# A hybrid decoder layer: two matmuls instead of three per weight tile in the mixer's projections by head, the halves copied by ScalarE and added by GpSimd

## The chip, the core and the metric

The kernel runs on one core of a Trainium2 chip. The metric is the device time of one execution in microseconds. Before the change it is 1942.86 us, the median of three runs (1942.37 to 1943.96).

## The reference

One layer with a sequence of T = 256 positions, model width D = 2048, heads of 128, eight attention heads ("fox") and eight recurrent heads ("gdn"):

```python
h = ada_in(x, norm_g[l, 0], sh1, sc1)                       # norm, scale and shift from c
x = x + 0.5 * gt1 * swiglu(h, gate_w[0], up_w[0], down_w[0])   # FFN 1
h = ada_in(x, norm_g[l, 1], sh2, sc2)
x = x + gt2 * hybrid_mixer(h, ...)                          # the mixer
h = ada_in(x, norm_g[l, 2], sh3, sc3)
x = x + 0.5 * gt3 * swiglu(h, gate_w[1], up_w[1], down_w[1])   # FFN 2
return rmsnorm(x, final_norm)

def hybrid_mixer(h, w_in, w_out, ...):
    q_f, k_f, v_f, f_f, qkv_g, a_g, b_g, z_g = split(h @ w_in)
    # fox: softmax(q k^T / sqrt(128) + decay(log_sigmoid(f_f))) @ v, then rmsnorm
    # gdn: qkv_g -> causal conv of width 4 -> silu -> q, k, v;
    #      q and k normed, gates from a_g and b_g,
    #      gated delta rule in chunks of 64 (a triangular solve per chunk), times silu(z)
    return concat(o_f, o_g) @ w_out
```

## The kernel before, in words

**Products.** The activations stand transposed, features on the partitions. Weights come from memory in blocks of eight tiles of 128x128 (one DMA of 512 KB, L121). Each number is split into a high and a low part: ScalarE (ACT) casts a block to `whi` (L123), VectorE (DVE) takes the rest, `wlo` (L135), each with four buffers. The activations are split likewise into halves HI and LO. A product is then high times high, plus high times low, plus low times high. In both FFNs and in the mixer's output projection most tiles are done by two matmuls: one of 512 columns, `whi` times both halves of the activations side by side (L481, L485), and one of 256, `wlo` times HI (L482, L486). In the mixer's projections by head, `project` (L760 to L773) does three matmuls of 256 columns per tile (L769, L770, L771) into the same 256 columns of a PSUM bank `pp`, and the sum of the three is there when the last has run. There are 41 such projections of 16 tiles, 656 tiles in all: gates, 8 keys, 16 queries and values of gdn, 16 queries and keys of fox. The projections Z and V run over rows instead (L782 to L784, three of 512 columns).

**Stages.** FFN 1 takes the span's first 738 us, the mixer runs to about 1235, FFN 2 to the end. The mixer starts with one `project` of four heads (64 tiles: gates and keys 0 to 2), and then follows a list written by hand, `ORDER`: K3 ... K7 Z0 V0 F0 G0 F1 G1 ... F7 (K keys, G the queries and values of a gdn head, F queries and keys of a fox head). Then comes the output projection (`po`, L485 and L486), and FFN 2.

**Small work.** Everything behind a projection is a generator: `gates`, `keys`, `decays`, `solve`, `gdn`, `fox`, `to_out`. Each stops at `yield n` and is taken up once the clock of `tick`, 0.35 us a tile, has moved on by n. So the places of its matmuls in PE's queue are fixed when the program is built, in tiles, and PE runs its queue in order: a small matmul whose input isn't ready holds all products behind it. A scheduler puts the instructions of each of the other engines in order, and these too run in that order.

**After a projection.** `conv_silu` (L915) copies `pp` into `cp` (ACT L918), scales it (ACT L919), adds three shifted taps (DVE L921) and applies silu (ACT L922). `gates` (L799) copies 24 rows (ACT L802); a matmul turns them (`pcol`, L811), DVE and ACT work on the result (L813 to L835), `prow` and `pcum` sum it (L844 to L853), ACT L855 copies the row sums, which go to memory (`rowd`) and come back spread over the partitions (`x<-rowd`, `rw<-rowd`). From these `decays` builds `Ln` (DVE L902, then eight exponentials on ACT, L905), which the last step of `keys` (DVE L947) multiplies. `keys` itself does transposes (`pk`, L934), products (`pkk`, L937), and then ACT L940 and L941, with PSUM tiles that the next head's `keys` uses again. `fox` gets its `qk` by two ACT copies (L1241).

Of the kernel before, what the change touches and what calls it, by code (L numbers as in the profile page):

```python
# [8 lines left out]
F32 = mybir.dt.float32  # L9
# [3 lines left out]
AF = mybir.ActivationFunctionType  # L13
ALU = mybir.AluOpType
PSUM = bass.MemoryType.PSUM

P = 128
D = 2048
T = 256
KD = D // P  # L20
# [5 lines left out]
NH = 8  # L26
HD = 128
# [3 lines left out]
GR = 24  # L31
# [44 lines left out]
def woven(ap):  # L76

    return ap.rearrange("p (a b) -> p b a", a=2)


def runs(ap):

    return ap.rearrange("p (a b) -> p a b", a=2)


def turns(ap):

    return ap.rearrange("p (b a) -> p a b", a=2)
# [61 lines left out]
def layer_kernel(ctx: ExitStack, tc: tile.TileContext, xrow, c, adaw, cols, cst, w, out, order, dbg=None):  # L150
    nc = tc.nc
    V, A, G, PE = nc.vector, nc.scalar, nc.gpsimd, nc.tensor
# [200 lines left out]
    LO, HI = 0, 1  # L353
# [312 lines left out]
    for kind, i in (("x", 0), ("x", 1), ("c", 0), ("c", 1), ("x", 2), ("x", 3), ("c", 2), ("c", 3)):  # L666
        with nullcontext() if hold is None else tc.issue_after(hold):
            if kind == "c":
                hold = cond(i)
            else:  # L670
                t, q = divmod(i, 2)
# [57 lines left out]
    def mixer():  # L729
# [30 lines left out]
        def project(items):  # L760

            pp = [psn(i, "pp") for i in range(len(items))]
            todo = [(i, k) for k in range(KD) for i in range(len(items))]
            for i, k in todo:
                m, n = items[i]
                h_need(k)
                wh, wl = W.next(m, k, n)
                hh, hl = woven(plain[:, k, HI]), woven(plain[:, k, LO])
                PE.matmul(pp[i][:, :T], wh, hh, start=(k == 0), stop=False)  # L769
                PE.matmul(pp[i][:, :T], wh, hl, start=False, stop=False)  # L770
                PE.matmul(pp[i][:, :T], wl, hh, start=False, stop=(k == KD - 1))  # L771
                tick(TILE_US)
            return [p_[:, :T] for p_ in pp]  # L773

        def project_rows(mat, grp):

# [22 lines left out]
        def gates(ps):  # L799

            yr = x[:, 8]
            A.copy(runs(yr[R]), turns(ps[R]))  # L802
            y, ny, e, em, t0, q = (x[:, j, : 2 * GR].rearrange("p (t r) -> p t r", t=2) for j in range(10, KD))
            coef = tiny.tile([P, GR + PAD["hid"]], F32, name="coef", bufs=1)[:, :GR]
            tc.keep_in_program_order(A.activation(coef, L("alog"), AF.Exp))
            V.tensor_scalar(coef, coef, -1.0, None, ALU.mult)
            yield 2.0
            pc = psf("pcol")
            pcv = pc[:, : 2 * GR].rearrange("p (t r) -> p t r", t=2)
            for t in range(2):  # L810
                PE.transpose(pcv[:, t], yr[R, t * P : (t + 1) * P], ident[R, :GR])  # L811
            both = lambda c_: c_.unsqueeze(1).to_broadcast([P, 2, GR])
            V.tensor_tensor(y, pcv, both(L("gbias")), ALU.add)  # L813
            V.tensor_tensor(y, y, both(C("sgn")), ALU.mult)
            V.scalar_tensor_tensor(ny, y, -1.0, y, ALU.mult, ALU.min)
            A.activation(e, ny, AF.Exp)
            V.tensor_scalar(em, y, 0.0, None, ALU.min)
            A.activation(em, em, AF.Exp)

            S = ny  # L820
            V.tensor_scalar(t0, e, 2.0, None, ALU.add)
            V.reciprocal(t0, t0)
            V.tensor_tensor(S, e, t0, ALU.mult)
            V.tensor_tensor(t0, S, S, ALU.mult)
            V.tensor_scalar(q, t0, 1.0 / 17.0, None, ALU.mult)
            for n in (15, 13, 11, 9, 7, 5, 3):
                V.scalar_tensor_tensor(q, q, 1.0 / n, t0, ALU.add, ALU.mult)
            V.scalar_tensor_tensor(q, q, 1.0, S, ALU.add, ALU.mult)
            V.tensor_scalar(y, y, 0.0, None, ALU.max)
            V.scalar_tensor_tensor(y, q, 2.0, y, ALU.mult, ALU.add)  # L830
            V.tensor_tensor(y, y, both(coef), ALU.mult)

            V.tensor_scalar(t0, e, 1.0, None, ALU.add)
            V.reciprocal(t0, t0)
            V.tensor_tensor(colS[:, :, 4], em[:, :, 16:24], t0[:, :, 16:24], ALU.mult)  # L835
            yield 8.0

            fox_, gdn_ = slice(0, NH), slice(NH, 2 * NH)
            pr = psf("prow")
            po = psf("pcum")  # L840
            pcs = po[:, : 6 * NH].rearrange("p (t q r) -> p t q r", t=2, q=3)
            for t in range(2):
                sl = slice(t * P, (t + 1) * P)
                PE.matmul(pr[:NH, T + t * P : T + (t + 1) * P], y[:, t, gdn_], C("tri64"), start=True, stop=True)  # L844
                PE.matmul(pr[:NH, sl], y[:, t, fox_], C("tri"), start=True, stop=(t == 0))
                if t:
                    PE.matmul(pr[:NH, sl], y[:, 0, fox_], L("ones"), start=False, stop=True)
            for t in range(2):
                PE.matmul(pcs[:, t, 1], C("tri64"), y[:, t, gdn_], start=True, stop=True)
                PE.matmul(pcs[:, t, 2], C("tru64"), y[:, t, gdn_], start=True, stop=True)  # L850
                PE.matmul(pcs[:, t, 0], C("tri"), y[:, t, fox_], start=True, stop=(t == 0))
                if t:
                    PE.matmul(pcs[:, t, 0], L("ones"), y[:, 0, fox_], start=False, stop=True)  # L853
            rt = x[:, 8:10].rearrange("p a t -> p (a t)")[:NH]
            A.copy(rt, pr[:NH])  # L855
            nc.sync.dma_start(rows, rt)
            V.tensor_copy(colS[:, :, 0:2], pcs[:, :, 0:2])
            A.activation(colS[:, :, 2:4], pcs[:, :, 1:3], AF.Exp)
            V.tensor_tensor(nbeg, colS[:, :, 4], colS[:, :, 2], ALU.mult)
            V.tensor_scalar(nbt, colS[:, :, 4], -1.0, None, ALU.mult)  # L860
            V.tensor_scalar(ng, colS[:, :, 1], -1.0, None, ALU.mult)
            yield 2.0
            fetch_rows(0)
            yield 1.0
# [50 lines left out]
        def conv_silu(ps, n, dst):  # L915
            cp, cv = pt("cp"), pt("cv")
            tap = lambda s: L("conv", 4 * n + s, 1)
            A.copy(runs(cp), turns(ps))  # L918
            A.activation(cv, cp, AF.Copy, scale=tap(3))  # L919
            for s in range(1, 4):  # L920
                V.scalar_tensor_tensor(cv[:, s:], cp[:, : T - s], tap(3 - s), cv[:, s:], ALU.mult, ALU.add)  # L921
            A.activation(dst, cv, AF.Silu)  # L922
# [3 lines left out]
        def keys(h):  # L926

            kT = kk[h].bitcast(F32)
            yield 3.0
            pk = pss("pk")  # L930
            pg = pss("pkk")
            for t in range(2):
                sl = slice(t * P, (t + 1) * P)
                PE.transpose(pk[:, sl], kT[:, 0, sl], ident)  # L934
            for t in range(2):
                sl = slice(t * P, (t + 1) * P)
                PE.matmul(pg[:, sl], kT[:, 0, sl], kT[:, 0, sl], start=True, stop=True)  # L937
            for t in range(2):
                j1 = tmp.tile([P, P], BF16, name="j1")
                A.activation(j1, pk[:, t * P : (t + 1) * P], AF.Square, accum_out=ssk[:, t, h : h + 1])  # L940
            A.copy(kT[:, 1], pk[:, :T])  # L941
            V.tensor_scalar(ssk[:, :, h], ssk[:, :, h], EPS, None, ALU.add)
            V.reciprocal(r2[:, :, h], ssk[:, :, h])
            nb2 = tiny.tile([P, 2], F32, name="nb2")
            V.tensor_tensor(nb2, nbt[:, :, h], r2[:, :, h], ALU.mult)
            for t in range(2):
                V.scalar_tensor_tensor(Ln[:, h, t], pg[:, t * P : (t + 1) * P], nb2[:, t : t + 1], Ln[:, h, t], ALU.mult, ALU.mult)  # L947
# [50 lines left out]
        def gdn(h):  # L998
# [1 line left out]
            kT, q_ = kk.pop(h).bitcast(F32), qv.pop(h).bitcast(F32)  # L1000
            dec, egb = ups.pop(h)
            L_, U = Ln[:, h], U0[:, h]
            yield 5.0 if h < NH - 2 else 3.0

            pv = pss("pvq")
            pg = pss("pkq")
# [136 lines left out]
        def fox(h, qk, vt):  # L1143
# [2 lines left out]
            for t, o, wd in ((0, 0, P), (1, P, T)):  # L1146
                A.activation(fm[:, o : o + wd], cb[:, :wd], AF.Identity, bias=colS[:, t, 0, h : h + 1], scale=-1.0)
            V.tensor_tensor(fm, fm, C("foxm"), ALU.add)
            yield 1.0
            pl = psf("plog")  # L1150
            for t, o, wd in ((0, 0, P), (1, P, T)):
                sl = slice(t * P, (t + 1) * P)
# [51 lines left out]
        def step(kind, h):  # L1204
# [25 lines left out]
            elif kind == "V":  # L1230
                finish("k", NH if h else 0)
                pv = project_rows("vf", h)
                vts[h] = [spare(4 * h), spare(4 * h + 2)]
                for t in range(2):
                    A.copy(vts[h][t], pv[t])
            else:
                pp = [project([(m, h)])[0] for m in ("qf", "kf")]
                finish("fox", h - 1)
                qk = spare(8 + 2 * (h % 2)).rearrange("p (a t) -> p a t", a=2)
                for i in range(2):  # L1240
                    A.activation(runs(qk[:, i]), turns(pp[i]), AF.Copy, scale=1.0 / math.sqrt(HD) if i == 0 else 1.0)  # L1241
                start("fox", h, fox(h, qk, vts[h // 4]))
                if h + 1 < NH:
                    rowf[h + 1] = row_of(h + 1, 0, "f")
# [200 lines left out]
```

## Time and profile before

| | us |
|---|---|
| median of three runs | 1942.86 (1942.37 to 1943.96) |
| the profiled execution | 1943.79 |
| its span | 1941.9, so 1.9 lie around the span |
| busy: PE, PE weight loads | 1903.0, 1777.2 |
| busy: DVE, ACT, GpSimd (POOL) | 1554.0, 1041.2, 56.8 |
| granted clock of TensorE | 0.992 |

The page gives busy time by engine, 40 slices of the span, the chain that ended last and the costliest groups of instructions. A group's line has the source line, the engine, the operation, output and inputs, the count, and then the busy time in us and the mean of one in ns; matmuls are pipelined, so the mean of one is longer than the distance from one start to the next. That distance is read from the timeline, whose first column is the start in us and whose second is the duration. A row of the waits names who waited, for whom, for how long in all, how often, and the longest.

### The profile page before, as it was taken

The numbers are of one execution on the slowest core, as the hardware profiler recorded it, in microseconds if no ns is written. First come the engines' busy times: TensorE is split into PE (matmuls) and PEld (weight loads), VectorE is DVE, ScalarE is ACT, GpSimd is POOL, SyncE is SP. The second block draws the span as 40 slices with busy tenths as digits, with TensorE's granted clock in tenths as the row PEclk, the third lists the DMA queues.
The fourth block names the chain that finished last, engine by engine and source line by source line (L and its number), as shares of the span: only waits on it lengthen the run. The fifth ranks groups of instructions, "written<-read, shape, count | busy, mean of one in ns | idle before, by whom it ended". The sixth has DMA issues, their size and how long they took to land. (4 is left out here: it accounts for less than half of the span.)

```text
span 1941.9 us, 33701 instructions
## 1 busy us (share of the span) xinstructions
PE 1903.0 (98%) x13087; PEld 1777.2 (92%) x13087; DVE 1554.0 (80%) x2415; ACT 1041.2 (54%) x1647; POOL 56.8 (3%) x55
## 2 busy tenths in 40 slices
PE   8999999999999999999999999999999999999998
PEld 6999999998999988889989998999999999999997
DVE  6999978989989997779987989976777665666654
ACT  6544555433455446858657655665554445555553
POOL 0000000000000030000000001100000000000011
PEclk8999999999999999999999999999999999999999
DMA  9989867999999975586667568667767665565663
GB/s 371 359 308 358 305 224 258 400 369 376 356 358 339 361 302 212 212 314 220 214 242 257 201 218 303 208 258 252 245 253 257 244 225 200 201 200 202 202 200 120
DMA packets 129490, 519.58 MB, mean 268 GB/s; under 512 B 18217, under 2 KB 21545, under 8 KB 111153
## 3 DMA queue, kind: packets, MB, share of 16 engines
q1 hardware_dynamic: 129330, 517.42, 72.9%
q8 instruction: 103, 1.69, 0.3%
q14 instruction: 57, 0.47, 0.1%
HBM read 512.89 MB, written 4.47 MB: 266 GB/s over the span
## 5 line engine op out<-in xcount | busy, mean ns | idle before, releaser
L135 DVE TENSOR_TENSOR wlo<-wraw,whi 128x1024 fp32r<-128x1024 f32 x674 | 822.3, 1226 | 268.3 <-ACT whi L123 267.3
L123 ACT CAST whi<-wraw 128x1024 fp32r<-128x1024 f32 x674 | 700.6, 1047 | 515.1 <-PE pd L485 166.5
L485 PE MATMUL pd<-hid,whi 128*128 128x512 f32 x1408 | 461.8, 382 | 0.0
L486 PE MATMUL pd<-hid,wlo 128*128 128x256 f32 x1408 | 384.6, 273 | 2.6 <-DVE wlo L135 2.6
L260 DVE CUSTOM_DVE_ANT_0 adat<-adat,cs,colt 128x2048 f32<-128x2048 f32 x140 | 329.2, 2351 | 6.5 <-DMA adat<-in_ada_dram 6.5
L481 PE MATMUL pg<-hs,whi 128*128 128x512 f32 x912 | 302.2, 382 | 0.5 <-DVE shc L432 0.5
L481 PE MATMUL pu<-hs,whi 128*128 128x512 f32 x912 | 302.2, 382 | 0.0
L485 PEld LDWEIGHTS pd<-hid,whi 128*128 128x128 f32 x1408 | 266.0, 189 | 36.9
L486 PEld LDWEIGHTS pd<-hid,wlo 128*128 128x128 f32 x1408 | 270.3, 192 | 5.4 <-DVE wlo L135 5.3
L567 PE MATMUL pgu<-hs,whi 128*128 128x256 f32 x896 | 245.8, 277 | 5.9 <-ACT hs L371 5.9
L482 PE MATMUL pu<-hs,wlo 128*128 128x256 f32 x912 | 249.2, 273 | 0.0
L482 PE MATMUL pg<-hs,wlo 128*128 128x256 f32 x912 | 248.9, 273 | 0.0
L569 PE MATMUL pgu<-hs,wlo 128*128 128x256 f32 x896 | 245.1, 278 | 2.4 <-DVE wlo L135 2.4
L568 PE MATMUL pgu<-hs,whi 128*128 128x256 f32 x896 | 246.5, 277 | 0.0
L481 PEld LDWEIGHTS pg<-hs,whi 128*128 128x128 f32 x912 | 172.4, 189 | 24.8 <-ACT shc L431 0.7
L481 PEld LDWEIGHTS pu<-hs,whi 128*128 128x128 f32 x912 | 172.4, 189 | 23.6
L769 PE MATMUL pp<-hs,whi 128*128 128x256 f32 x656 | 188.9, 289 | 1.6 <-ACT hs L375 1.6
L770 PE MATMUL pp<-hs,whi 128*128 128x256 f32 x656 | 182.9, 279 | 0.0
L771 PE MATMUL pp<-hs,wlo 128*128 128x256 f32 x656 | 182.7, 278 | 0.0
L567 PEld LDWEIGHTS pgu<-hs,whi 128*128 128x128 f32 x896 | 172.9, 194 | 6.7 <-ACT hs L371 6.3
L482 PEld LDWEIGHTS pu<-hs,wlo 128*128 128x128 f32 x912 | 175.0, 192 | 1.0 <-DVE wlo L135 0.9
L482 PEld LDWEIGHTS pg<-hs,wlo 128*128 128x128 f32 x912 | 175.1, 192 | 0.4
(337 smaller groups left out, 2593.8 us busy)
## 6 DMA issues: line engine op xcount, KB each, us to landing
wraw<-in_w_dram SPq DMA_DIRECT2D x674, 512.0 KB, 4.4
adat<-in_ada_dram SPq DMA_DIRECT2D x140, 1024.0 KB, 7.2
xr<-in_xr_dram SPq DMA_DIRECT2D x4, 512.0 KB, 5.3
adaf<-in_ada_dram SPq DMA_DIRECT2D x4, 512.0 KB, 8.5
adaf<-in_ada_dram SPq DMA_DIRECT2D x2, 1024.0 KB, 12.3
xd<-x SPq DMA_DIRECT2D x4, 512.0 KB, 7.0
rw<-rowd SPq DMA_DIRECT2D x16, 128.0 KB, 4.3
x<-xd SPq DMA_DIRECT2D x4, 512.0 KB, 5.8
```

Source lines behind the costliest of these rows:

```text
L123: self.cast = self.nc.scalar.copy(self.h, r).ins
L135: lo_ = nc.vector.tensor_tensor(self.l, r, self.h.bitcast(F32), ALU.subtract)
L260: V.tensor_tensor_reduce(t, t, cs, 1.0, L("adab", q, 1), ALU.mult, ALU.add, mod[:, q : q + 1])
L481: PE.matmul(ps, wt[0], both, start=(k == 0), stop=False)
L482: PE.matmul(ps[:, T:], wt[1], part(k, HI), start=False, stop=(k == KD - 1))
L485: PE.matmul(ps, wt[0], act.rearrange("p q (a b) -> p q b a", a=2), start=first, stop=False)
L486: PE.matmul(ps[:, :T], wt[1], woven(act[:, 0]), start=False, stop=last)
L567: PE.matmul(o, wh, part(k, HI), start=first and s == 0, stop=False, skip_group_check=skip)
L568: PE.matmul(o, wh, part(k, LO), start=False, stop=False, skip_group_check=skip)
L569: PE.matmul(o, wl, part(k, HI), start=False, stop=last, skip_group_check=skip)
L769: PE.matmul(pp[i][:, :T], wh, hh, start=(k == 0), stop=False)
L770: PE.matmul(pp[i][:, :T], wh, hl, start=False, stop=False)
```

## The change

`project` does one matmul of 512 columns (both halves of h) and one of 256 per tile. The bank `pp` then holds two partial sums of 256 columns. A new function `summed` brings them together: ACT copies all 512 columns into a tile `cb`, GpSimd adds the two halves of `cb` into the destination. `cb` is in a pool with one buffer. It replaces the ACT copy of 256 columns in `gates`, `conv_silu` and `fox`. The first `yield` of `keys`, `gdn` and the one of `fox` ahead of its `plog` are 1.5 longer.

```diff
@@ project
-                hh, hl = woven(plain[:, k, HI]), woven(plain[:, k, LO])
-                PE.matmul(pp[i][:, :T], wh, hh, start=(k == 0), stop=False)
-                PE.matmul(pp[i][:, :T], wh, hl, start=False, stop=False)
-                PE.matmul(pp[i][:, :T], wl, hh, start=False, stop=(k == KD - 1))
+                both = plain[:, k].rearrange("p q (a b) -> p q b a", a=2)
+                PE.matmul(pp[i], wh, both, start=(k == 0), stop=False)
+                PE.matmul(pp[i][:, T:], wl, both[:, HI], start=False, stop=(k == KD - 1))
                 tick(TILE_US)
-            return [p_[:, :T] for p_ in pp]
+            return pp
+
+        def summed(dst, ps, n=P, scale=1.0):
+            cb = m1p.tile([P, 2, T], F32, name="cb")
+            A.activation(cb[:n].rearrange("p q (a b) -> p q a b", a=2), ps[:n].rearrange("p (q b a) -> p q a b", q=2, a=2),
+                         AF.Copy, scale=scale)
+            G.tensor_tensor(dst, cb[:n, 0], cb[:n, 1], ALU.add)
@@ gates
-            A.copy(runs(yr[R]), turns(ps[R]))
+            summed(yr[R], ps, GR)
@@ conv_silu
-            A.copy(runs(cp), turns(ps))
+            summed(cp, ps)
@@ keys
-            yield 3.0
+            yield 4.5
@@ gdn
-            yield 5.0 if h < NH - 2 else 3.0
+            yield 6.5 if h < NH - 2 else 4.5
@@ fox
-            yield 1.0
+            yield 2.5
@@ step, F
-                    A.activation(runs(qk[:, i]), turns(pp[i]), AF.Copy, scale=1.0 / math.sqrt(HD) if i == 0 else 1.0)
+                    summed(qk[:, i], pp[i], scale=1.0 / math.sqrt(HD) if i == 0 else 1.0)
```

In the changed program the lines behind `project` have numbers higher by 6: L918 of before is L777 with L779, L919 is L925, L921 L927, L922 L928, L902 L908, L905 L911, L937 L943, L941 L947. Three places show how queues move with it.

The first is ACT's queue where the first projection of four heads ends. Before:

```order
L802 COPY x<-pp 24x256
L805 ACT_TABLE_LOAD
L805 ACTIVATE coef<-colt 128x24
L918 COPY cp<-pp 128x256
L123 CAST whi<-wraw 128x1024
L919 ACTIVATE cv<-cp,colt 128x256
L918 COPY cp<-pp 128x256
L919 ACTIVATE cv<-cp,colt 128x256
```

In the changed program, at the same place:

```order
L777 ACTIVATE cb<-pp 128x512
L123 CAST whi<-wraw 128x1024
L925 ACTIVATE cv<-cp,colt 128x256
L777 ACTIVATE cb<-pp 128x512
L925 ACTIVATE cv<-cp,colt 128x256
L777 ACTIVATE cb<-pp 128x512
L123 CAST whi<-wraw 128x1024
L928 ACT_TABLE_LOAD
L928 ACTIVATE kk<-cv 128x256
L777 ACTIVATE cb<-pp 24x512
```

The copy of the gates (24 rows) stood first and now stands tenth, behind the copies of the three keys, two casts, two scalings and a table load; each L777 can start once the GpSimd add before it has read the one `cb`. On PE, the transposes `pcol`, which need the gates' sum, stood behind 73 weight tiles of the mixer and now stand behind 83 and a half; `prow` stood behind 112 tiles and now behind 99 and a half.

The second place is DVE's queue around the subtraction that builds `Ln` for heads 0 to 3 (L902, now L908), whose input comes by DMA from `rowd`. Before, and then in the changed program:

```order
L135 TENSOR_TENSOR wlo<-wraw,whi 128x1024 x2
L921 SCALAR_TENSOR_TENSOR cv<-cp,colt,cv 128x255
L942 TENSOR_SCALAR ssk<-ssk 128x2
L921 SCALAR_TENSOR_TENSOR cv<-cp,colt,cv 128x254
L902 TENSOR_TENSOR Ln<-cstt,x 128x1024
L921 SCALAR_TENSOR_TENSOR cv<-cp,colt,cv 128x253
L943 RECIPROCAL r_8262<-ssk 128x2
L135 TENSOR_TENSOR wlo<-wraw,whi 128x1024
```

In the changed program:

```order
L135 TENSOR_TENSOR wlo<-wraw,whi 128x1024
L927 SCALAR_TENSOR_TENSOR cv<-cp,colt,cv 128x255
L908 TENSOR_TENSOR Ln<-cstt,x 128x1024
L927 SCALAR_TENSOR_TENSOR cv<-cp,colt,cv 128x254
L135 TENSOR_TENSOR wlo<-wraw,whi 128x1024
L927 SCALAR_TENSOR_TENSOR cv<-cp,colt,cv 128x253
L887 TENSOR_TENSOR dec<-cstt,rw 128x256
```

The subtraction stood behind the `wlo` of the block that starts with tile 136; it now stands ahead of the `wlo` for tile 128.

The third place is ACT's queue at the exponentials behind that subtraction. Before:

```order
L123 CAST whi<-wraw 128x1024
L1147 ACTIVATE fm<-rw,colS 128x128
L905 ACT_TABLE_LOAD
L905 ACTIVATE Ln<-Ln,colS 128x128 x8
L922 ACT_TABLE_LOAD
L922 ACTIVATE kk<-cv 128x256
L940 ACTIVATE j_9047,ssk<-pk 128x128
L940 ACTIVATE j_9049,ssk<-pk 128x128
L941 COPY kk<-pk 128x256
```

In the changed program:

```order
L911 ACT_TABLE_LOAD
L911 ACTIVATE Ln<-Ln,colS 128x128 x2
L928 ACT_TABLE_LOAD
L928 ACTIVATE kk<-cv 128x256
L911 ACT_TABLE_LOAD
L911 ACTIVATE Ln<-Ln,colS 128x128 x6
L777 ACTIVATE cb<-pp 128x512
L123 CAST whi<-wraw 128x1024
L925 ACTIVATE cv<-cp,colt 128x256
L946 ACTIVATE j_8890,ssk<-pk 128x128
L946 ACTIVATE j_8892,ssk<-pk 128x128
L947 COPY kk<-pk 128x256
```

The exponentials stood behind the cast and behind the first head's L940 and L941; they now stand ahead of the cast for the block that starts with tile 136 and ahead of the first head's L946 and L947. The second head's `pkk`, which uses that head's PSUM tile again, stood behind 144 tiles and now stands behind 136 and a half.

## The prediction

> **What bounds the kernel now.** I read the page first (busy time by engine, then the chain that ended last), then the waits of PE and the windows inside the mixer, then timelines. The page, engine by engine, and the chain's shares:
>
> ```profile
> PE 1903.0 (98%) x13087; PEld 1777.2 (92%) x13087; DVE 1554.0 (80%) x2415; ACT 1041.2 (54%) x1647; POOL 56.8 (3%) x55
> ...
> PE 37%; DVE 2%; issue 1%; ACT 0%; DMA 0%; SPq 0%; DVEq 0%; ACTq 0%
> ```
>
> PE is busy 98% of 1941.9 us. So a shorter product shows in the time, and so does every idle moment of PE that the change adds: 5 us of PE waiting undo 5 us of faster products. DVE with its 80% is the engine next to the limit, and an average hides where it is full. The mixer by stretches, columns busy us and count for PE, weight loads, DVE, ACT, POOL, then granted clock, DMA share, GB/s; the first two rows hold PE and its clock alone:
>
> ```profile
> 771.20:807.40 36.20, 36.20 (x305) 1.00 0.62 229
> 807.40:816.00 8.60, 5.87 (x23) 0.80 0.34 121
> 885.00:960.00 75.00, 73.48 (x634) 71.50 (x633) 72.52 (x215) 53.82 (x128) 0.00 (x0) 1.00 0.65 220
> ```
>
> From 771.2 to 807.4, while gates and keys are worked out, PE doesn't lose anything (36.20 of 36.20). Right behind it comes the mixer's one large loss. From 885 to 960 DVE has 2.5 us free of 75. PE's longest waits between 740 and 1178, in all, times, longest:
>
> ```profile
> PE pkk L937 <- ACT kk L941: 2.7, 1, 2.7
> PE pft L1189 <- issue: 1.4, 1, 1.4
> PE ppt L1167 <- ACT x L1162: 1.3, 2, 1.1
> PE pot L1133 <- DVE orw L1124: 1.0, 2, 0.6
> PE po L1103 <- DVE vz L1101: 1.0, 2, 0.7
> ```
>
> All these are small products that stand in PE's queue at a place fixed in tiles and whose input is late.
>
> **The products (the gain).** Ten tiles of the mixer's three matmuls and thirteen of the output projection's two, first start and last; both read the activations with the same strides:
>
> ```profile
> 769.57 0.28 PE L769 MATMUL pp<-hs,whi 128*128 128x256 f32 x1
> ...
> 772.92 0.28 PE L769 MATMUL pp<-hs,whi 128*128 128x256 f32 x1
> ...
> 1159.94 0.38 PE L485 MATMUL po<-oh,whi 128*128 128x512 f32 x1
> 1160.16 0.27 PE L486 MATMUL po<-oh,wlo 128*128 128x256 f32 x1
> ...
> 1164.20 0.38 PE L485 MATMUL po<-oh,whi 128*128 128x512 f32 x1
> ...
> L769 PE MATMUL pp<-hs,whi 128*128 128x256 f32 x656 | 188.9, 289 | 1.6 <-ACT hs L375 1.6
> ```
>
> Three matmuls take 3.35/10 = 0.335 us a tile, two take 4.26/13 = 0.328. The saving is 0.007 us a tile (the rounding of the starts leaves 0.0065 to 0.0085), over 656 tiles **-5.0 us** (-4.3 to -5.6). The number of columns is the same, 768 a tile; what goes is one start per tile. The Trainium skill (TensorE: Matmul & The Clock Gate, Back-to-back issue gap) gives the isolated distance as N/2.4 + 2.5 ns, so one start less would be worth 2.5 ns a tile; the trace has 7 ns, and by the page alone the gain would be an estimated 1.6 us.
>
> **The copies and adds.** One copy of 256 columns becomes one of 512 and a GpSimd add. Rows: the old copy, a 512-column copy out of PSUM, the fox copy (count, duration ns min/median/max), and the add of two 128x256 tiles that GpSimd already does for the norms:
>
> ```profile
> L918 ACT COPY cp<-pp x24: 347/356/398, 772.9 to 1111.7; 128x256 f32<-128x256 f32 x24
> L1241 ACT ACTIVATE x<-pp x16: 366/378/392, 857.4 to 1144.5; 128x256 f32<-128x256 f32 x16
> L580 ACT COPY acc<-pgu x28: 568/587/619, 33.4 to 66.9; 128x512 f32<-128x512 f32 x28
> L313 POOL TENSOR_TENSOR sqacc<-sqacc,sq x42: 727/1142/2257, 669.1 to 1924.1; 128x256 f32<-128x256 f32 x42
> ```
>
> ACT gets 41 x 0.23 = 9 us more in a stretch where it has a quarter or more free (53.82 of 75): nothing by itself. GpSimd is nearly empty, 41 adds of 1.1 to 2.3 us fit. What costs is the delay: a summed tile is ready 0.23 + 1.1 to 2.3, so 1.4 to 2.5 us later than a copied one, and through the one buffer `cb` each L777 waits for the add before it. The yields that are 1.5 longer pay for this in the later steps, in `gates` nothing does.
>
> **The first stretch (the loss).** Rows of ACT and PE before, where the gates' chain starts, and of the wait that is there now:
>
> ```profile
> 771.11 0.36 ACT L802 COPY x<-pp 24x256 f32<-24x256 f32 x1 [0.74 <-PE pp L771]
> 773.16 1.05 ACT L123 CAST whi<-wraw 128x1024 fp32r<-128x1024 f32 x1
> 774.11 0.51 ACT L919 ACTIVATE cv<-cp,colt 128x256 f32<-128x256 f32 x1
> 775.02 0.30 PE L811 MATMUL pcol<-colt,x 24*128 24x24 f32 x2
> 776.38 1.28 ACT L922 ACT_TABLE_LOAD   x1
> L922 ACT ACTIVATE qv<-cv x16: 405/416/422, 878.8 to 1118.1; 128x256 f32<-128x256 f32 x16
> 788.51 0.39 PE L844 MATMUL prow<-cstt,x 128*8 128x128 f32 x2
> 800.61 1.22 DVE L902 TENSOR_TENSOR Ln<-cstt,x 128x1024 f32<-128x1024 f32 x1
> 805.43 2.45 ACT L905 ACTIVATE Ln<-Ln,colS 128x128 f32<-128x128 f32 x8
> 807.30 0.38 PE L934 MATMUL pk<-colt,kk 128*128 128x128 f32 x2
> 810.42 0.71 PE L937 MATMUL pkk<-kk 128*128 128x128 f32 x4 [2.73 <-ACT kk L941]
> 811.62 0.62 PE L782 MATMUL pv<-whi,hs 128*128 128x512 f32 x1
> 812.04 0.63 PE L783 MATMUL pv<-wlo,hs 128*128 128x512 f32 x1
> ```
>
> Now the gates' copy is ACT's first, done at 771.47, 3.5 us ahead of `pcol`. In the changed order it is the tenth. I add up what stands ahead of it from about 770.6 (64 tiles x 0.007 earlier): three L777 of 0.59, two casts of 1.05, two scalings of 0.51, a table load of 1.28, one silu of 0.42, and what ACT waits for the first adds, an estimated 1.0: 7.6, so it starts at 778 to 779, and with its own copy, the add and the handing on (0.6 + 1.1 to 2.0) `pcol` can start at 780 to 781.5. PE comes to it behind 83.5 tiles at about 777.7 (83.5 - 64 = 19.5 tiles x 0.328 = 6.4 behind 771.3). **PE waits 3.0 us** (2 to 4) where it waited none. Since 771.2 to 807.4 has no idle time of PE at all, nothing swallows it.
>
> The rest of that chain: from `pcol` to `prow` DVE and ACT took 13.5 us (775.02 to 788.51), with conv taps and three `wlo` among it; now DVE has the chain's steps together, some 7 us, and PE has 16 tiles, 5.2 us, and one block's `wlo` stands behind them: **1.0** at `prow`, **0.3** for the `wlo` behind. `rowd` then goes to memory and back, which took from 788.51 to 800.61, 12.1 us. DVE now has that subtraction ahead of the `wlo` of tile 128; PE comes there at about 801 and the landing is no earlier than 788 + 12 = 800, with 1.22 for the subtraction and 1.22 for the `wlo`: **1.5**. Then ACT's eight exponentials, now with two table loads more among them (2.45 + 2 x 1.28 + 0.42), and an L777 stand ahead of the cast for tile 136: cast at 808, `wlo` at 810, PE there at 805.5: **4.5**. The second `pkk`, half a block later, waits for the first head's copy, behind that cast: **1.9**. And a wait of 2.7 us now is followed by starts 0.42 us apart (811.62 to 812.04) instead of 0.216, in a window with clock 0.80; eight such starts, **1.7**. Sum 13.9. What the old order pays here goes: the gap at 807.30 to 810.42 (3.0) and its 1.7 of slow clock. Net **+9.2** (4 to 14, since each term leans on the one before it).
>
> On that slow clock the page just named (Part 1, the HAM clock gate) has the clock fall to half after an idle window of about 3.4 us; here 2.7 us have been enough, so the trace differs. By the page only the longest of these waits would do it.
>
> **The middle and the tail.** `ppt` (1.3) may go, since the exponentials of heads 4 to 7 move too; `pft` grows by about 0.7. GpSimd's adds also slow DVE. Rows:
>
> ```profile
> L135 DVE TENSOR_TENSOR wlo<-wraw,whi x674: 1200/1224/1683, 22.5 to 1920.1; 128x1024 fp32r<-128x1024 f32 x169
> L409 DVE SCALAR_TENSOR_TENSOR hs<-x,g,hs x16: 480/968/1032, 1175.3 to 1237.0; 128x256 fp32r<-128x256 f32 x16
> ```
>
> L135 goes from 1.22 to 1.68 at most and L409 from 0.48 to 0.97; both maxima lie beside L313. So an add costs DVE up to 0.46, and nothing where DVE has no such work beside it; the middle is 0.23. With 8 adds between 885 and 960 that is 0 to 3.7 us against 2.5 free, and the conv taps that wait for adds come on top: I take 1.6 for what shows, net **+1.0** (-2 to +6). The Trainium skill (GPSIMD Engine Reference, Key points) says that GpSimd shares its memory interfaces with VectorE and collides with instructions that have two SBUF inputs; L135 is one, and these maxima agree. At the mixer's end the last `summed` sits ahead of the last fox heads, whose waits are under 1 us each now: **+0.8** (0 to 2).
>
> **The sum.** -5.0 + 9.2 + 1.0 + 0.8 = +6.0 us. The profiled execution took 1943.79 (span 1941.9 and 1.9 around it), 0.9 above the median; the terms are differences, so I put the sum on the median: 1942.86 + 6.0 = 1948.9 us. FFN 2 behind the mixer has PE full and hands a shift on unchanged. A measurement of this kernel tells about 0.2%, 3.9 us, from no change.
>
> **Rivals.**
> - *The waits are hidden.* If the adds take 1.1 us and ACT runs the first stretch without waiting, `pcol` waits under 1 us, the chain shifts earlier, and the old wait at `pkk` with its slow clock goes too (4.7), in place of the new ones of about the same size. Then the product's gain is what is left: 1942.86 - 5.0 = 1937.9. For it: the whole gain is a plain row-by-row difference, and the old order pays 4.7 here. Against it: the gates' copy behind nine instructions, and PE without slack there. It decides when the new stalls up to tile 168 come to under 6 us. 0.19.
> - *They cancel.* Half the new stalls (9 instead of 13.9) leave 1942.86 - 5.0 + 4.3 + 1 = 1943. 0.24.
> - *DVE is full in the middle.* 32 adds behind the first stretch at 0.23 to 0.46 are 7 to 15 us of DVE, and conv taps stand in its queue waiting for adds. If half shows: 1948.9 + 6 = 1955. Against: outside 885 to 960 DVE has a fifth of its time free. 0.12.
> - *A shorter gain.* The rows of 0.335 and 0.328 stand in different stages. If two thirds of the difference belong to the place (what else loads the memory there) and only a third to the start that goes, the gain is 1.7 instead of 5.0 and the time 1952.2. That both forms read the same strides speaks against it; 0.03. The Trainium skill's distance of N/2.4 + 2.5 (same page and section) would make it about this.
> - *The products don't get faster at all,* because a bank with two partial sums waits longer for its copy: `pp` is copied in 0.59 instead of 0.36, with a step of 5.2 us between two projections. 0.01, about 1954.
>
> My forecast has 0.41, its own range is 1946.8 to 1953. Slower by over 0.2% (above 1946.7): 0.41 + 0.12 + 0.03 + 0.01 = 0.57; within: 0.24; faster: 0.19. The range that holds 8 in 10 reaches from the hidden waits to the lower part of the full DVE, 1937 to 1955.
>
> **What would show it.** L769 and L770 0.328 apart per tile; PE waiting at `pcol` (L817) for POOL some 3 us at about 778; the old `pkk` wait smaller; a `wlo` wait (L770 for DVE) of several us between 800 and 812, and starts 0.42 us apart behind it; DVE rows of L135 with more maxima of 1.68; POOL with 41 adds, some 50 us more. The forecast is wrong if PE stays fully busy up to tile 136, or if its waits between 885 and 1143 grow by more than 3 us.

## The result and the profile after

The changed kernel takes 1959.28 us, the median of five runs (1957.01 to 1962.31), against 1942.37 before, five runs as well (1939.1 to 1943.96): ratio 1.0085, 95% interval 1.0073 to 1.0097, so 16.5 us slower. The forecast was 1948.9 with a range of 1937 to 1955: the sign was right, the size was not.

The page of the changed kernel, busy times by engine and the two lines of the product:

```profile
span 1960.5 us, 32493 instructions
PE 1905.9 (97%) x12430; PEld 1754.7 (90%) x12431; DVE 1568.0 (80%) x2415; ACT 1054.7 (54%) x1650; POOL 97.5 (5%) x96
...
L769 PE MATMUL pp<-hs,whi 128*128 128x512 f32 x656 | 235.2, 402 | 6.7 <-ACT whi L123 4.4
L770 PE MATMUL pp<-hs,wlo 128*128 128x256 f32 x656 | 185.4, 283 | 0.0
```

POOL has 41 instructions more, as forecast, and 40.7 us, where some 50 were forecast. DVE has 14 us more with the same number of instructions, 2415: its instructions have become longer.

Where the time went is read from the same three tiles in both kernels. I counted PE's matmuls from the mixer's start; the timeline rows are tile 0, tile 168 (24 tiles into Z0, whose rows also name `pv`; each row of its first product stands for two tiles) and tile 960 (in the output projection), first before, then after:

```profile
747.46 0.58 PE L769 MATMUL pp<-hs,whi 128*128 128x256 f32 x1 [1.55 <-ACT hs L375]
817.13 0.46 PE L782 MATMUL pv<-whi,hs 128*128 128x512 f32 x1
1163.87 0.38 PE L485 MATMUL po<-oh,whi 128*128 128x512 f32 x1
```

```profile
749.14 0.76 PE L769 MATMUL pp<-hs,whi 128*128 128x512 f32 x1 [2.28 <-DVE hs L376]
824.22 0.46 PE L788 MATMUL pv<-whi,hs 128*128 128x512 f32 x1
1182.61 0.38 PE L485 MATMUL po<-oh,whi 128*128 128x512 f32 x1
```

From tile 0 to 168 the change adds 75.08 - 69.67 = 5.4 us, from 168 to 960 358.39 - 346.74 = 11.7, behind that nothing (777.9 to the span's end against 778.0). Another 1.7 stand ahead of tile 0, where nothing was changed, between these two executions. So two thirds of the loss lie in the middle, where the prediction had +1.0 and, at its end, +0.8. The same stretch as a window, before and after (its length, PE's busy time and count, clock, DMA share, GB/s):

```profile
817.13:1163.87 346.74, 339.81 (x2587) 1.00 0.67 238
824.22:1182.61 358.39, 339.71 (x2083) 1.00 0.66 235
```

PE is busy for the same time in both, although its products became shorter, and its idle time grew from 6.9 to 18.7 us, by as much as the stretch itself.

PE's waits in the changed kernel's mixer behind tile 0 (in all, times, longest):

```profile
PE pp L769 <- ACT whi L123: 4.4, 1, 4.4
PE po L1106 <- DVE st L1117: 2.9, 3, 2.1
PE pfo L1179 <- ACT x L1175: 2.3, 1, 2.3
PE pot L1139 <- DVE Z L1035: 2.1, 3, 1.1
PE po L1109 <- DVE vz L1107: 2.0, 4, 0.8
PE pvq L1021 <- ACT qv L928: 1.9, 1, 1.9
PE pcol L817 <- POOL x L779: 1.7, 1, 1.7
...
PE plog L1159 <- POOL x L779: 1.0, 1, 1.0
```

Before, the longest was 2.7. Now there is one large wait for a cast (`whi`), and many shorter ones at small products that wait for DVE or ACT. Only `pcol` and one `plog` wait for GpSimd itself.

**The hold.** Two stretches of the changed kernel's timeline in the middle, DVE and POOL:

```profile
966.64 0.73 POOL L779 TENSOR_TENSOR x<-cb 128x256 f32<-128x256 f32 x1 [2.63 <-ACT cb L777]
966.70 0.68 DVE L286 TENSOR_TENSOR rsa_o<-rsy_o 128x2 f32<-128x2 f32 x1
...
985.18 0.17 DVE L284 TENSOR_SCALAR rsa_f<-fss 128x2 int32<-128x2 int32 x1
985.34 0.74 POOL L779 TENSOR_TENSOR cp<-cb 128x256 f32<-128x256 f32 x1 [7.44 <-DVE rsa_f L284]
985.38 0.73 DVE L285 TENSOR_SCALAR rsy_f<-rsa_f 128x2 int32<-128x2 int32 x1
986.14 0.16 DVE L286 TENSOR_TENSOR rsa_f<-rsy_f 128x2 f32<-128x2 f32 x1
```

L285 and L286 work on two numbers a partition and take 0.16 to 0.17 us. The one that starts just behind an add takes 0.68 or 0.73 and ends when the add ends (966.70 + 0.68 = 967.38 against 966.64 + 0.73 = 967.37; 985.38 + 0.73 = 986.11 against 986.08). It doesn't run slower, it stands still until GpSimd is through.

Not every DVE instruction is held. Beside another add of the changed kernel, a reduction of one tile in SBUF (L982) and a copy out of PSUM (L1115) take no longer than elsewhere:

```profile
944.22 0.74 POOL L779 TENSOR_TENSOR cp<-cb 128x256 f32<-128x256 f32 x1 [8.45 <-ACT cb L777]
944.36 0.15 DVE L982 TENSOR_REDUCE x<-x 64x4 f32<-64x16 f32 x1
944.43 0.27 DVE L1115 COPY st<-pst 128x128 f32<-128x128 f32 x1
```

The Trainium skill (GPSIMD Engine Reference, Key points) has the shared memory interface collide with DVE instructions that have two SBUF inputs or a two-port mode. L286 has two such inputs, and the trace agrees. The two that aren't held have one SBUF input at most, and so has L285, which is held; which of these run in a two-port mode no trace here shows.

**The order on ACT.** The changed kernel's timeline of ACT ahead of tile 136, and PE there:

```profile
799.64 1.03 ACT L123 CAST whi<-wraw 128x1024 fp32r<-128x1024 f32 x1
800.68 1.28 ACT L911 ACT_TABLE_LOAD   x1
801.98 0.69 ACT L911 ACTIVATE Ln<-Ln,colS 128x128 f32<-128x128 f32 x2
802.68 1.28 ACT L928 ACT_TABLE_LOAD   x1
803.97 0.42 ACT L928 ACTIVATE kk<-cv 128x256 f32<-128x256 f32 x1
804.39 1.28 ACT L911 ACT_TABLE_LOAD   x1
805.69 1.86 ACT L911 ACTIVATE Ln<-Ln,colS 128x128 f32<-128x128 f32 x6
807.93 1.03 ACT L123 CAST whi<-wraw 128x1024 fp32r<-128x1024 f32 x1
...
809.01 0.79 PE L769 MATMUL pp<-hs,whi 128*128 128x512 f32 x1 [4.37 <-ACT whi L123]
811.05 0.63 PE L769 MATMUL pp<-hs,whi 128*128 128x512 f32 x1
811.47 0.42 PE L770 MATMUL pp<-hs,wlo 128*128 128x256 f32 x1
...
803.00:824.00 21.00, 16.19 (x71) 0.84 0.48 174
```

Three table loads, a silu and eight exponentials stand between two casts, 7.3 us. PE waits 4.37 and then starts 512 columns 0.42 apart (811.05 to 811.47) with a clock of 0.84 in the window.

### The profile page after: what moved, and what is told of

Its sections match the earlier page's. It is cut to its first block, busy times and chain, and to the rows that moved or that the text cites. A ratio compares the mean times of both kernels' runs of the same rounds, so it can differ in the third digit from the quotient of the medians.

```text
span 1960.5 us, 32493 instructions
## 1 busy us (share of the span) xinstructions
PE 1905.9 (97%) x12430; PEld 1754.7 (90%) x12431; DVE 1568.0 (80%) x2415; ACT 1054.7 (54%) x1650; POOL 97.5 (5%) x96
## 5 line engine op out<-in xcount | busy, mean ns | idle before, releaser
L135 DVE TENSOR_TENSOR wlo<-wraw,whi 128x1024 fp32r<-128x1024 f32 x674 | 823.4, 1229 | 271.3 <-ACT whi L123 267.2
L769 PE MATMUL pp<-hs,whi 128*128 128x512 f32 x656 | 235.2, 402 | 6.7 <-ACT whi L123 4.4
L569 PEld LDWEIGHTS pgu<-hs,wlo 128*128 128x128 f32 x896 | 172.3, 194 | 3.3 <-DVE wlo L135 3.3
```

The costliest lines, as they stand in the source:

```text
L135: lo_ = nc.vector.tensor_tensor(self.l, r, self.h.bitcast(F32), ALU.subtract)
L569: PE.matmul(o, wl, part(k, HI), start=False, stop=last, skip_group_check=skip)
L769: PE.matmul(pp[i], wh, both, start=(k == 0), stop=False)
```

## The experiments

Ratios are to the kernel before, with 95% intervals; 0.001 is 1.9 us. Four theories: **places** (the longer yields), **hold** (a GpSimd add stops DVE), **lateness** (the sums come later), **order** (the queues stand worse, on ACT above all).

**The parts one by one.** `product_only` is the kernel before with

```diff
-                PE.matmul(pp[i][:, :T], wh, hh, ...)
-                PE.matmul(pp[i][:, :T], wh, hl, ...)
-                PE.matmul(pp[i][:, :T], wl, hh, ...)
+                PE.matmul(pp[i], wh, both, start=(k == 0), stop=False)
+                PE.matmul(pp[i][:, T:], wl, both[:, HI], start=False, stop=(k == KD - 1))
```

> The kernel before with the product of 512 columns alone: ACT copies only the first 256 columns as before, so the parts high-low and low-high, which stand in the other half, are left out of the result; no GpSimd, old yields. All theories: the products' gain without its price, 5 us less than before (ratio 0.9974, 1937.4 against 1942.4). If the product itself gains only a third of that, 1.7 us less (0.9991).

Measured 0.9968 (0.9957 to 0.9978), 6.2 us less. The product's gain is there. In the trace, tiles without a wait stand 0.3275 us apart, before 0.334; over 656 tiles that is 4.4 us. The rest shows around the old wait at `pkk`, 1.7 us here instead of 2.7: between tiles 144 and 168, where no product changed, the kernel gains 2.5 us.

`yields_only` is the kernel before with the three longer yields.

> The kernel before with nothing but the three yields 1.5 longer. Theory places (the longer yields move the small steps into each other, and that costs): 5 to 11 us over before (1.0026 to 1.0057). Theory delay: the inputs are ready earlier than needed, so -1 to +3 us (0.9995 to 1.0015), the wait at pkk with its slow clock perhaps gone.

Measured 1.0000 (0.9991 to 1.0009). Places by themselves cost nothing in all. But they move time: in the trace (one execution, as in all readings by tile), tile 0 to 168 takes 63.8 us, 5.9 less than before, with no idle time of PE and without the wait at `pkk`, and tile 168 to 960 takes 351.4, 4.6 more.

`extra_adds` puts an add that nobody reads behind each of the old copies:

```diff
             A.copy(runs(cp), turns(ps))
+            G.tensor_tensor(jg, cp, cp, ALU.add)
```

> The kernel before with 41 GpSimd adds of 128x256 (24 partitions for the gates) more, one behind each copy, whose result nobody reads. Theory contention (GpSimd's adds slow DVE, which is full in the middle): 7 to 15 us over before (1.0036 to 1.0077). Theory delay (what costs is that a summed tile is later, not that GpSimd is busy): 0 to 1.5 us over before (1.000 to 1.0008), with L135 maxima of 1.68 us all the same.

Measured 1.0044 (1.0032 to 1.0057), 8.5 us more, with no result of GpSimd on any path. By the traces ACT's and DVE's instructions stand in the same order as before, so the order on them plays no part, and the cost lies in the middle: tile 0 to 168 takes 67.6 us, 2.0 less than before, and 168 to 960 takes 353.1, 6.4 more. Its timeline, DVE and POOL:

```profile
950.46 2.34 DVE L260 CUSTOM_DVE_ANT_0 adat<-adat,cs,colt 128x2048 f32<-128x2048 f32 x1
950.72 2.55 POOL L802 TENSOR_TENSOR jg<-x 128x256 f32<-128x256 f32 x1 [6.87 <-ACT x L1248]
952.73 0.56 DVE L290 SCALAR_TENSOR_TENSOR rsa_o<-rsa_o,sso 128x2 f32<-128x2 f32 x1
```

The exclusion goes both ways: the add issued at 950.72 sits through DVE's long instruction, and then holds the next one (0.56 instead of 0.16) until it ends at 953.27.

`extra_small` is the same with 8 columns per add.

> The kernel before with the 41 unread GpSimd adds over 8 columns instead of 256. If an add costs DVE a fixed hold per GpSimd instruction: about as with 256 columns, 5 to 8 us over before (1.0025 to 1.004), and DVE instructions 0.3 to 0.4 us too long beside each. If the cost goes with the elements that GpSimd moves (two engines sharing a memory port): 0 to 1 us (1.000 to 1.0005).

Measured 1.0001 (0.9992 to 1.0009). ACT's and DVE's order is the same again. The hold lasts as long as the add moves data, it isn't a fixed price per instruction. The same step, with such an add issued behind the same long instruction:

```profile
948.96 2.35 DVE L260 CUSTOM_DVE_ANT_0 adat<-adat,cs,colt 128x2048 f32<-128x2048 f32 x1
949.19 2.17 POOL L802 TENSOR_TENSOR jg<-x 128x8 f32<-128x8 f32 x1 [7.46 <-ACT x L1248]
951.23 0.16 DVE L290 SCALAR_TENSOR_TENSOR rsa_o<-rsa_o,sso 128x2 f32<-128x2 f32 x1
```

The add of 8 columns sits through the long instruction too, ends with the small step behind it, and that step takes its usual 0.16.

`adds_only` is the changed kernel with high-high into one half of `pp` and the two other products, 256 columns each, into the other.

> The changed kernel with three matmuls of 256 columns again, high-high into the one half of the bank and the two others into the other half: all of the price (copy of 512, GpSimd add, longer yields), none of the gain. If gain and price add up: 5 us over the changed kernel, some 22 us over before (ratio 1.0113, 1964). If the faster products themselves bring the small steps too early, and so make part of the price: at or under the changed kernel (1.006 to 1.0085).

Measured 1.0071 (1.0058 to 1.0084): with slower products it is no slower than the changed kernel, where 5 us more were expected. Gain and price don't add up; its order on ACT has no large wait at tile 136.

**The engine.** `dve_from_cb` changes one word:

```diff
-            G.tensor_tensor(dst, cb[:n, 0], cb[:n, 1], ALU.add)
+            V.tensor_tensor(dst, cb[:n, 0], cb[:n, 1], ALU.add)
```

> The changed kernel with one word changed: DVE instead of GpSimd adds the two halves of cb. One cb, the 512-column copy, the place of the gates on ACT and the longer yields stay. Theory engine (GpSimd's own slowness, 0.6 to 1.3 us against some 0.4, and its hold on DVE make most of the price): 12 to 18 us under the changed kernel, ratio to before 0.999 to 1.002. Theory buffer (the one cb and the 512-column copy hold ACT up, whoever adds): 6 us or less under the changed kernel, 1.0055 and up.

Measured 0.9969 (0.9957 to 0.9981): 6 us faster than before and 22 faster than the changed kernel, better than either theory gave. The one buffer, the 512-column copy and the gates' late place on ACT stay, so none of these makes the loss by itself. The page's first lines, and ACT at the exponentials:

```profile
span 1934.5 us, 32448 instructions
...
806.65 0.37 ACT L947 COPY kk<-pk 128x256 f32<-128x256 f32 x1
807.92 0.80 ACT L1153 ACTIVATE fm<-rw,colS 128x128 f32<-128x128 f32 x2 [0.89 <-DMA rw<-rowd]
808.74 1.28 ACT L911 ACT_TABLE_LOAD   x1
810.03 2.45 ACT L911 ACTIVATE Ln<-Ln,colS 128x128 f32<-128x128 f32 x8
```

Here the eight stand together behind one table load, and the first head's copy (L947) is ahead of them. The scheduler laid the queues out otherwise because DVE, not GpSimd, adds. So the 22 us hold both, the engine that adds and the order that comes with it.

`dve_merge` adds straight from PSUM, behind an ACT copy of the first half; `dve_keys` and `dve_old` are the same with the longer yield in `keys` alone and in none.

```diff
+            A.activation(runs(dst), turns(ps[:n, :T]), AF.Copy, scale=scale)
+            V.scalar_tensor_tensor(runs(dst), turns(ps[:n, T:]), scale, runs(dst), ALU.mult, ALU.add)
```

> The changed kernel without GpSimd: ACT copies the first 256 columns into the destination, DVE adds the other 256 straight from PSUM; products of 512 and longer yields stay. Theory hold (each GpSimd instruction holds up the DVE instruction that starts with it by some 0.4 us, in the serial chains that PE waits for) together with theory delay (a sum that is ready 1 to 2 us later): most of the 23 us of price go, 2 to 8 us under before (ratio 0.996 to 0.999). Theory full DVE (41 more DVE instructions of 0.48 us, 20 us, in a stretch with few us free): 5 us or more over before (1.0026 and up).

> ACT copies one half, DVE adds the other from PSUM (as dve_merge), with the longer yield in keys alone; gdn and fox have their old ones. A sum made so is 0.5 us later than a copy, so gdn and fox need no longer yield, and in keys it takes away the wait at pkk and its slow clock: 4 to 8 us under before (0.996 to 0.998). If the longer yields of gdn and fox are needed: as dve_merge or worse (0.9984 and up).

> As dve_merge with all three old yields. If the wait at pkk (4.6 us with its slow clock) stays with the old yield of keys: 2 to 4 us over dve_keys (0.998 to 1.000). If yields don't matter: as dve_keys.

Measured 0.9984 (0.9976 to 0.9993), 0.9987 (0.9978 to 0.9995) and 0.9976 (0.9966 to 0.9987). All are faster than before; 41 more DVE instructions are borne, so a full DVE isn't what costs. The three intervals overlap, and the forecast on the yields wasn't borne out.

`dve_cb_old` is `dve_from_cb` with the old yields.

> dve_from_cb with the three old yields. As between dve_merge and dve_old, the yields are worth little: 0 to 2 us under dve_from_cb (0.996 to 0.997). If the copy of 512 makes the sums late enough to need them: 2 to 5 us over it (0.998 to 0.9995).

Measured 0.9998 (0.9989 to 1.0007), 5.6 us over `dve_from_cb`: with the copy of 512 columns the longer yields are needed.

**Hold or lateness.** `dve_hold` is `dve_from_cb` with an unread GpSimd add of the same halves beside DVE's; `dve_late` is `dve_from_cb` with four GpSimd adds of 8 columns that DVE's add has to wait for.

```diff
+            G.tensor_tensor(jg[:n], cb[:n, 0], cb[:n, 1], ALU.add)              # dve_hold
+            for _ in range(4):                                                  # dve_late
+                G.tensor_tensor(dst[:, :8], cb[:n, 0, :8], cb[:n, 1, :8], ALU.add)
             V.tensor_tensor(dst, cb[:n, 0], cb[:n, 1], ALU.add)
```

> dve_from_cb (DVE adds) with a GpSimd add of the same two halves beside it, whose result nobody reads. The hold without the lateness. If the hold costs on the new products what it did on the old ones (8 us with 41 unread adds): 6 to 10 us over dve_from_cb, ratio to before 1.000 to 1.002. If the hold is nearly all of the price of GpSimd: 18 us or more over dve_from_cb, 1.006 and up.

> dve_from_cb with four GpSimd adds of 8 columns into the destination ahead of DVE's add, which overwrites it and so waits for them, some 1 us: the lateness without the hold. If lateness makes the rest of the price: 8 to 14 us over dve_from_cb (ratio to before 1.001 to 1.004). If a sum that is 1 us later costs nothing by itself: within 3 us of dve_from_cb (0.9985 and less).

Measured 1.0026 (1.0016 to 1.0036) and 1.0046 (1.0033 to 1.0058): the hold costs 11 us over `dve_from_cb`, and sums that come later cost 15. In `dve_hold` ACT's and DVE's instructions stand in the order of `dve_from_cb`; it isn't free of lateness, since DVE's own adds are held too and the median sum is ready 1.94 us behind the start of its copy instead of 1.47. But the changed kernel's sums are not later than those of `dve_from_cb`: from the start of the copy to the end of the sum the medians over 41 sums are 1.46 and 1.47 us (in `dve_late` 2.63), since DVE's add stands in a queue that is often busy. So lateness would cost, but isn't what parts these two kernels. That theory falls for the changed kernel.

**The order in the first stretch.** `f_and_g` has the new form in F and G alone, `gates_old` everywhere but in the gates, and `two_cb` copies the halves one by one, the first into the destination, with two smaller buffers.

> The new form in the 32 projections of F and G alone; gates and keys with three matmuls, an ACT copy and their old yield. If the loss of the first stretch (some 6 us net up to tile 168) and that of the middle (some 11 us) add up: 10 to 12 us over before (1.0051 to 1.0062). If the lateness of the first stretch is what shifts the middle: 3 us or less over before (1.0015).

> The changed kernel with the gates alone, one projection of 41, by three matmuls of 256 and one ACT copy as before. Theory queue (the gates' sum, tenth on ACT, pushes the whole chain to the exponentials ahead of the cast for tile 136): the 4.5 us at tile 136 and the wait at pcol go, 5 to 7 us under the changed kernel, ratio to before 1.005 to 1.0065. Theory hold alone: nothing but one add less, as the changed kernel (1.008 to 1.009).

> The changed kernel with the copy in two halves of 256, the first into the destination, the second into cb, which now has two buffers in the same memory; GpSimd adds as before. On ACT the gates' first copy stands first again. Theory buffer: 10 us or more under the changed kernel (ratio to before 1.0035 and less). Theory engine: the hold and the late sums stay, only a part of the first stretch's loss goes: 2 to 6 us under the changed kernel (1.0055 to 1.0075).

Measured 1.0036 (1.0025 to 1.0048), 1.0065 (1.0053 to 1.0077) and 1.0037 (1.0025 to 1.0049). F and G cost 7 us net, between the two cases, which leaves 9.5 for gates and keys if the parts add up. The gates alone are worth 3.9 of these, a little under the 5 to 7 expected; in that trace PE no longer waits at `pcol`, but still waits 3.2 us for a cast, so the jam on ACT only became smaller. `two_cb` gains 9 us with GpSimd still adding, close to what the theory of the buffer gave: between 770 and 830 PE waits for no cast there. As long as GpSimd adds, the way the halves are copied matters too.

`late_decays` lets the first `decays` wait 11.0 instead of 5.0.

> The changed kernel with one number changed: the first decays yields 11.0 instead of 5.0, so that the subtraction from rowd and the eight exponentials stand some 17 tiles later in the program, behind the cast for tile 136. GpSimd still does all 41 adds. Theory order (the exponentials with their table loads ahead of the cast for tile 136 are some 7 to 10 us of the price): 5 to 9 us under the changed kernel (ratio to before 1.004 to 1.006). If the jam only moves to the next block: within 2 us of the changed kernel (1.0075 to 1.0095).

Measured 1.0090 (1.0072 to 1.0108). The jam moved by a block, as the second case had it:

```profile
PE pv L788 <- ACT whi L123: 5.2, 1, 5.2
```

`exps_together` ties the exponentials to the last silu instead:

```diff
+                    with tc.issue_after(silu[-1]) if half == 0 else nullcontext():
-                    A.activation(Ln[:, h, t], ...)
+                        A.activation(Ln[:, h, t], ...)
```

> The changed kernel with the first eight exponentials told to stand behind the last silu issued so far. On ACT they then stand together, with one table load ahead of them instead of three, behind the cast for tile 136 and the first head's L946 and L947. GpSimd still does all 41 adds. Theory order: the 4.4 us at tile 136 and the slow clock behind it go, 5 to 9 us under the changed kernel (ratio to before 1.004 to 1.006). If the jam moves again, as it did with late_decays: within 2 us of the changed kernel (1.0075 to 1.0095).

Measured 1.0057 (1.0043 to 1.0071), 5.4 us under the changed kernel. PE's waits there between 775 and 830:

```profile
PE pcol L817 <- POOL x L779: 1.3, 1, 1.3
...
PE pv L788 <- ACT whi L123: 0.4, 1, 0.4
```

The wait for the cast went from 4.4 to 0.4, and tile 0 to 168 takes 68.0 us instead of 75.1. This part of the loss is order: silu and exponentials in turns on ACT, a table load at each turn.

**What the runs add up to.** The product -6; GpSimd in place of DVE +22 (1.0085 against 0.9969). The hold is some 11 where it was measured (`dve_hold`, in another order) and the order on ACT some 5 (`exps_together`). If these add up, which no run shows, 6 us are open: the wait at `pcol`, other places in the order, and the interaction of these were not taken apart. In the profiled executions, which lie 3 us further apart than the medians, 11.5 us fall between tile 0 and 168 and 13.3 between 168 and 960; of the latter the hold makes 7.3 (`dve_hold` over `dve_from_cb`).

## Why the prediction was wrong

- **The gain** was right: -5.0 forecast, -6.2 measured (-4.3 to -8.4 by the interval). The pace of the tiles, on which the forecast stood, makes 4.4 of it; that the total came out above 5.0 is luck, by a shorter wait at `pkk` that the term didn't count.
- **The first stretch** was right in its mechanism, somewhat too large in size: +9.2 less some 1 of product gain, measured 5.4 from tile 0 to 168. The largest term, 4.5 us at tile 136 behind exponentials and table loads, came out as 4.37. `pcol` waited 1.7 instead of 3.0, `pkk` 0.4 instead of 1.9, and the waits at `prow` and tile 128 didn't show in the list of waits. What the old order paid there went, as forecast (4.7; `yields_only` gains 5.9 in this stretch).
- **The middle and the tail** is the step that failed: +1.8 forecast, 11.7 measured from tile 168 to 960, and that with the product's gain in it (512 of the tiles in between, at 0.0067 us each, 3.4 us). The prediction's own sign of being wrong, waits in the middle that grow by over 3 us, came: PE's idle time grew by 11.8. The prediction had the right rows (L135 from 1.22 to 1.68, L409 from 0.48 to 0.97) but read them as a longer instruction on a busy engine, and set 8 adds against 2.5 us that DVE has free. DVE's free time wasn't the measure. In the middle PE waits for short serial chains on DVE (`vz`, `st`, `Z`, and what follows the square root steps L284 to L292), and a hold of 0.5 us on an instruction of 0.16 goes straight into such a chain, whether DVE is idle elsewhere or not. `extra_adds` priced this at 8.5 us, 6.4 of them by its trace in this stretch, where the step had 1.6. What makes the rest is open: the longer yields alone cost 4.6 there (`yields_only`), yet with DVE's adds they gain 1.4 there (`dve_from_cb` 345.1 us, `dve_cb_old` with the old yields 346.5).
- **The rivals.** "DVE is full in the middle" came nearest with 1955, but its mechanism is not what happened: `dve_merge` and `dve_from_cb` load DVE with 41 more instructions and are faster than before. The shorter gain, and products that don't get faster at all, are refuted by `product_only`; the hidden waits by the list of waits; that all cancels, by the 16.5 us.
- **Median and single runs:** the profiled execution of before was 0.9 above its median, that of after 3.0; the terms here are differences of spans and fit the medians to within 2 us.

## What to carry to other kernels

Before work goes to GpSimd because it is idle, look at what DVE does in those moments: a row of a small DVE instruction that takes several times its usual duration, and ends with a GpSimd instruction, is a hold, and its price is counted on the chain that waits for DVE, not on DVE's busy share. The same add on the "busier" engine can be much cheaper: one word was worth 22 us here, and `dve_from_cb` at 0.9969 beats both kernels. And where a scheduler sets the queues, a change of engine also changes the order: look in it for functions that take turns on ACT, since each turn is a table load of 1.28 us.

## What the runs showed of the hardware

A DVE instruction with two inputs in SBUF that starts during a GpSimd add of 128x256, once that add isn't itself waiting for DVE, stands still until the add is over, even if it handles two numbers a partition (0.16 became 0.56 to 0.68 us); so does a TENSOR_SCALAR on two numbers a partition (0.17 became 0.73). A reduction with one input and a copy out of PSUM run beside such an add at their usual 0.15 and 0.27. A GpSimd add issued during a long DVE instruction lasts until that is over (2.55 us against 0.6 to 0.75 alone). With 8 columns no hold shows in the row above, and no time is lost.

The length of a wait alone doesn't tell whether PE's clock drops behind it. It was low behind 2.7 us before and 4.4 us after (0.80 and 0.84 in the windows). Two more windows of the changed kernel (PE's busy time and count, clock, DMA share, GB/s) lie behind the waits of 2.3 us at `pfo` and 1.9 us at `pvq`:

```profile
885.00:893.00 8.00, 6.62 (x43) 1.00 0.83 329
1056.00:1064.00 8.00, 7.05 (x39) 0.79 0.87 328
```

The longer one left the clock at 1.00, the shorter one was followed by 0.79; there the low stretch itself, from 1058.1 to 1061.5, reads 0.50.
